# A two-block network in fp32: a head's rows come to all partitions by DMA and TensorE in place of GpSimd, and the merge's first branch is written three tiles ahead

## The chip, the cores and the metric

The kernel runs on one core of one Trainium2 chip. The metric is the device time of one execution in microseconds (us), as the median of several executions. Of the core's engines the text uses these names: PE (TensorE; PEld is its weight load), DVE (VectorE), ACT (ScalarE), POOL (GpSimd) and SP (SyncE, which here only issues DMAs).

## The reference

The reference is a two-block network over 512 tokens of width 1024, with 16 learned tokens put in front (528 columns in all). The change lies in the first block's token mixer, which has two branches from one input projection. Cut to them:

```python
y_a = gelu(s5_ssm(u, ...))                      # branch a: a state space model
y_a = y_a * sigmoid(y_a @ w_glu)
hb = mlstm_chunkwise(q, k, v, log_i, log_f)     # branch b: 4 heads of 128
hb = hb * rsqrt(mean(hb * hb, axis=-1) + eps) * g_head
y_b = hb * sigmoid(o)
merged = sigmoid(ga) * (y_a @ w_a) + sigmoid(gb) * (y_b @ w_b)
return x + rmsnorm(merged @ w_out, g_post)
```

In mlstm_chunkwise a score q.k of the tokens t and s is weighted by exp(F_t - F_s + log_i_s - m_t), F being the running sum of the log forget gates and m_t a running maximum; the result is divided by a normaliser by token.

## The kernel before, in words

All activations lie feature major: 128 features on the partitions, tokens along the free dimension. Products run in fp32r with each operand split into a high and a low half, so a product is three matmuls per 128 rows (`mm3`, lines 135 to 138, and `product`, lines 165 to 168). A chunk of weights (512 KB) is loaded by SP into one of three staging buffers (`wst`), copied to its high half by ACT (line 125) and to its low half by DVE (line 126), each with three buffers. PSUM banks for products come from `product_bank`: in phases with the extra pool in turns from that pool (tiles `mx`) and from the common one (tiles `mm`), else from the common one, every third time from the norms' bank (`rs`).

The mLSTM part (lines 793 to 835) treats the heads one after the other. `gate_rows` and `gate_scans` have already left, for the four heads, the negated running maximum in rows 0, 32, 64 and 96 of the tile `negm`. For a head, `mlstm_inputs` prepares q, k (convolution, tanh), v (transposed) and the output gate, and, as its last stage, has GpSimd copy the head's row of `negm` to all 128 partitions into the tile `nmb`, of which there is one (line 638). `mlstm_units` then works through eight pairs of a query range (258 or 256 columns) and a key tile: scores on PE; the decay as `nmb` plus a column per key on DVE (line 659), its exponential on ACT (line 660); where the key tile lies on the diagonal, a multiplication by a triangle on POOL (line 663); scores times decay on DVE (line 665); its split (lines 106 and 107); numerator and denominator on PE. The units' stages are woven with fillers: the products of the sixteen gate tiles and of the gated linear unit.

At the end, with two activations over the tile `rows` (lines 828 and 829), the norms' factors of the four heads stand in rows 0, 32, 64 and 96. For each head POOL copies its row to all partitions (line 832), DVE multiplies (line 834) and the result is split into `b2` (line 835). Then `merge`: for each of eight output tiles f it loads the chunk `w_ab[f]` and, for each of two token ranges, forms the product of branch a (from `a2`), its gating on DVE (line 893), the product of branch b (from `b2`), its gating, the sum of both on POOL (line 894) and the split (line 895). The loop is written tile by tile, a before b. After that come the inputs x, the bias rows of the second block (lines 1068 to 1078) and the product with `w_out`.

What is written is not the order in which the engines run: the framework's planner simulates the program and gives each engine a list in the order of the simulated times, keeping dependencies and buffers; each engine then works through its list in order, and so does SP with its DMAs. In the trace loads stand far ahead of their place in the text (the load of `rel`, line 1063, is issued at 213 us), and a tile waits for the release of the tile whose space it takes.

Of the kernel before, what the change touches and what calls it, by code (L numbers as in the profile page):

```python
# [49 lines left out]
# columns of the packed parameter vectors  # L50
# [13 lines left out]
class Net:  # L64
# [37 lines left out]
    def split(self, hi, lo, src, gain=None):  # L102
        """hi + lo = src * gain, each of 12 bits."""
        nc = self.nc
        if gain is None:
            nc.scalar.activation(hi, src, AF.Copy)
            nc.vector.tensor_tensor(lo, src, hi.bitcast(FT), OP.subtract)
        else:
            nc.scalar.activation(hi, src, AF.Copy, scale=gain)  # L109
            nc.vector.scalar_tensor_tensor(lo, src, gain, hi.bitcast(FT), OP.mult, OP.subtract)  # L110

    def weights(self, src, shape, own=None):
        """A chunk of weights [P, kt, cols] from DRAM as its two halves."""
# [16 lines left out]
    def mm3(self, ps, terms, start=True, stop=True):  # L130
        """ps (+)= sum of (ah + al)^T (bh + bl), leaving out al^T bl (2^-24 of the product)."""
# [8 lines left out]
    def project(self, w, c0, ranges, evac, m=P):  # L140
        """Columns c0.. of a weight chunk times the split activations, range by range."""
# [7 lines left out]
    def product(self, src, ranges, evac, m=P, after=None, own=None):  # L149
        """A chunk's product with the split activations as (load, pieces): evac(ps, t0, n) per range."""  # L150
# [23 lines left out]
    def product_bank(self):  # L174
        """A bank for a product: of the pool that all phases have, or in turns of that and more; in phases without
        wide norms, the norms' bank too, every third time."""
# [10 lines left out]
    def chain(self, jobs, last=None):  # L187
        """The pieces of jobs in order, each job's weights loaded one job ahead."""
# [8 lines left out]
    def log_exp_tables(self):  # L197
        """Of the function tables, those with both the logarithm and the exponential."""
# [8 lines left out]
    def next_input(self, act=None, extra=None, more=1):  # L207
        """Tiles for the next product's input, and for its tokens' factors; sums of squares in more parts where
        there's room for them."""
# [9 lines left out]
    def split_x(self, k, gname, t0, n):  # L219
        """Input tile k = x * g, split, and its part of the tokens' sums of squares."""  # L220
# [8 lines left out]
    def add_square(self, accs, x, k):  # L229
        """accs[k % len(accs)] (+)= x * x; the k-th of them."""  # L230
# [12 lines left out]
    def rstd(self, *a, **kw):  # L243
        """The steps of rstd_steps at once; returns the factors by token."""
# [4 lines left out]
    def rstd_wide(self, out, accs, t, width=DM):  # L249
        """out[:, t] = (sum over partitions of accs[..][:, t] / width + eps) ** -0.5 on every partition. One Newton  # L250
        step refines the tables' value."""
# [14 lines left out]
    def rstd_steps(self, pool, out, accs, n, width=DM, tag="rsr"):  # L266
        """out[:, t] = (sum over partitions of accs[..][:, t] / width + eps) ** -0.5 on every partition, for n
        tokens; and by token: [n / groups, groups]. One Newton step refines the tables' value."""
# [28 lines left out]
    def ssm_setup(self, pool, tmp):  # L297
        """Per state (partition: real or imaginary part, then state) and group: powers of lambda, the
        input matrix, and the rotations of the scan over chunks. A generator: lambda_bar, then the rest."""
# [56 lines left out]
        def cmul(orr, oi, ar, ai, br, bi, n):  # L356
            """(orr, oi) = a * b, with a of [P, n, NG] and b of [P, NG]."""
# [14 lines left out]
        # z = (lambda_bar - 1) / lambda  # L372
# [26 lines left out]
        # signed powers: al, be of the output side, qi of the input side  # L399
# [9 lines left out]
        # mag ** 8, and exp(i 8 theta c) as a product of two tables  # L409
# [26 lines left out]
    def ssm_tile(self, ft, ud, out):  # L436
        """One feature tile (8 groups) of the state space model as a generator: first its matrices,
        within a chunk (mt), from inputs to the chunk's state (q), from the state to outputs (pp); then
        2 gelu(y) to out, in the order of tokens."""
# [15 lines left out]
        # K[h', (lag, h)] of each group, and from it the block Toeplitz matrix  # L455
# [99 lines left out]
    def gate_rows(self, pool):  # L555
        """Rows 0, 32, 64, 96: the heads' running maximum (negated), exp(-2 m); and per key tile the
        columns a_s = log_i - F."""
# [14 lines left out]
    def gate_scans(self, pool, g8, li, zf):  # L572
# [21 lines left out]
        V.tensor_scalar(nm, nm, -1.0, None, OP.mult)  # L594
        ac = pool.tile([P, 5, 4], FT, name="acol")
# [7 lines left out]
    def mlstm_inputs(self, h, raws, ins):  # L603
        """q, k (convolved, split), v (by token, split) and tanh(o / 2) of one head, as a generator."""
# [32 lines left out]
        ins["m"] = self.hp.tile([P, L], FT, name="nmb")  # L637
        nc.gpsimd.partition_broadcast(ins["m"], self.negm[32 * h:32 * h + 1, :])

    def mlstm_units(self, h, ins, yb):  # L640
        """2 y_b of one head but for its norm's factor, and the factor's argument to a row: scores with
        their decays, a generator per key tile."""
# [54 lines left out]
    def mixer(self):  # L697
# [3 lines left out]
        with ExitStack() as es:  # L701
# [13 lines left out]
            with ExitStack() as e2:  # L715
# [4 lines left out]
                with tc.tile_pool(name="tmp0", bufs=1, side="right", reuse_waits="tile") as tmp:  # L720
# [26 lines left out]
                    # the factors are needed where a range's last piece ends  # L747
# [32 lines left out]
            def gate(f, out):  # L780
                """tanh(g / 2) of a gate's feature tile."""
# [11 lines left out]
            with ExitStack() as e2:  # L793
# [23 lines left out]
                load()  # L817
                for _ in prep(0):
                    pass
                units = []  # L820

                for h in range(4):
                    us = self.mlstm_units(h, ins[h], ybs[h])
                    units += ([prep(h + 1)] if h < 3 else []) + us
                self.weave([(units, fill)])
                # the heads' norms
# [1077 lines left out]
```

## Time and profile before

| what | value |
|---|---|
| device time, 3 runs | 1583.81, 1586.16, 1589.71 us; median 1586.16 us |
| profiled execution: its span, first to last instruction | 1585.8 us (the page lists no other time of it) |
| mean granted TensorE clock | 0.972 of full speed |
| busy: PE, DVE, ACT, POOL | 94%, 65%, 46%, 22% of the span |
| mLSTM with its fillers | about 217 to 377 us of the span |
| merge | about 377 to 430 us |

A line of the timeline gives the start in us from the span's start, the length in us, the engine, the line of the code, the operation, the tile written and those read, the shapes and a count of merged instructions; in square brackets stand the idle time of that engine just ahead, and what ended it ("issue": nothing that the profile shows). A PE row's length includes the pipeline's depth, so starts, not lengths, give its pace.

### The profile page before, as it was taken

The numbers are of one execution on the slowest core, as the hardware profiler recorded it, in microseconds if no ns is written. First come the engines' busy times: TensorE is split into PE (matmuls) and PEld (weight loads), VectorE is DVE, ScalarE is ACT, GpSimd is POOL, SyncE is SP. The second block draws the span as 40 slices with busy tenths as digits, with TensorE's granted clock in tenths as the row PEclk, the third lists the DMA queues.
The fourth block names the chain that finished last, engine by engine and source line by source line (L and its number), as shares of the span: only waits on it lengthen the run. The fifth ranks groups of instructions, "written<-read, shape, count | busy, mean of one in ns | idle before, by whom it ended". The sixth has DMA issues, their size and how long they took to land.

```text
span 1585.8 us, 24977 instructions
## 1 busy us (share of the span) xinstructions
PE 1485.1 (94%) x9745; PEld 1339.8 (84%) x9745; DVE 1031.2 (65%) x1960; ACT 722.4 (46%) x1396; POOL 341.0 (22%) x316
## 2 busy tenths in 40 slices
PE   5998998789998999999999999999889999999996
PEld 4988998778998999999999987878778888888886
DVE  8787877657777655555465687888888443344334
ACT  5233355446464533333455456666557441134332
POOL 4066720112343000000022354412343000000001
PEclk9998999989999999999999999999899999999998
DMA  5433331113645333233656322113230232323331
GB/s 187 95 97 104 80 107 50 54 41 120 213 146 160 107 93 94 93 95 91 190 162 197 119 67 67 52 56 107 81 107 28 93 93 94 93 93 94 93 93 54
DMA packets 65846, 160.86 MB, mean 101 GB/s; under 512 B 15032, under 2 KB 24488, under 8 KB 65600
## 3 DMA queue, kind: packets, MB, share of 16 engines
q1 hardware_dynamic: 64352, 156.65, 32.6%
q8 instruction: 76, 1.25, 0.3%
q0 software_dynamic: 288, 1.57, 0.3%
q10 hardware_dynamic: 1088, 1.05, 0.2%
q14 instruction: 42, 0.34, 0.1%
HBM read 152.84 MB, written 10.32 MB: 103 GB/s over the span
## 4 chain that ended last, share of the span: by engine, by line
PE 69%; DVE 18%; DMA 4%; ACT 4%; issue 4%; POOL 1%; SPq 0%; DVEq 0%; ACTq 0%; POOLq 0%
PE mm L135 6%; PE mm L138 6%; PE mm L136 6%; PE mm L165 6%; PE mm L168 6%; PE mm L167 6%; PE mx L168 5%; PE mx L165 5%; PE mx L167 5%; PE mx L135 2%; PE mx L136 2%; PE mx L138 2%; DVE wlo L126 2%; DVE xl L110 2%; PE mm L1324 1%
## 5 line engine op out<-in xcount | busy, mean ns | idle before, releaser
L126 DVE TENSOR_TENSOR wlo<-wst,whi 128x1024 fp32r<-128x1024 f32 (+2 forms) x227 | 283.2, 1249 | 197.4 <-ACT whi L125 121.6
L125 ACT ACTIVATE whi<-wst 128x1024 fp32r<-128x1024 f32 (+3 forms) x244 | 251.8, 1033 | 290.9 <-PE mm L136 94.6
L168 PE MATMUL mm<-xl,whi 128*128 128x256 f32 (+4 forms) x808 | 234.0, 315 | 0.3 <-DVE xl L110 0.3
L167 PE MATMUL mm<-xh,whi 128*128 128x256 f32 (+4 forms) x808 | 233.5, 314 | 0.2 <-DVE x L1614 0.2
L167 PE MATMUL mx<-xh,whi 128*128 128x512 f32 (+4 forms) x552 | 171.6, 332 | 8.1 <-ACT xh L109 7.5
L168 PE MATMUL mx<-xl,whi 128*128 128x512 f32 (+4 forms) x552 | 172.1, 332 | 3.2 <-DVE xl L110 3.2
L167 PEld LDWEIGHTS mm<-xh,whi 128*128 128x128 f32 (+1 forms) x808 | 154.1, 191 | 9.9 <-DVE x L1643 0.3
L168 PEld LDWEIGHTS mm<-xl,whi 128*128 128x128 f32 (+1 forms) x808 | 153.5, 190 | 10.3 <-issue 0.6
L165 PE MATMUL mm<-xh,wlo 128*128 128x256 f32 (+4 forms) x808 | 140.9, 314 | 0.0
L135 PE MATMUL mm<-hh,whi 128*128 128x256 f32 (+1 forms) x496 | 139.2, 311 | 0.0
L136 PE MATMUL mm<-hl,whi 128*128 128x256 f32 (+1 forms) x496 | 139.1, 310 | 0.0
L165 PEld LDWEIGHTS mm<-xh,wlo 128*128 128x128 f32 (+1 forms) x808 | 118.2, 190 | 9.7 <-issue 0.5
L167 PEld LDWEIGHTS mx<-xh,whi 128*128 128x128 f32 (+1 forms) x552 | 106.8, 193 | 17.7 <-ACT xh L109 7.7
L168 PEld LDWEIGHTS mx<-xl,whi 128*128 128x128 f32 (+1 forms) x552 | 106.7, 193 | 14.1 <-DVE xl L110 4.7
L165 PE MATMUL mx<-xh,wlo 128*128 128x512 f32 (+4 forms) x552 | 103.7, 329 | 0.0
L126 POOL TENSOR_TENSOR wlo<-wst,whi 128x1024 fp32r<-128x1024 f32 (+1 forms) x34 | 75.0, 2209 | 123.1 <-PE mm L138 38.3
L966 POOL TENSOR_TENSOR acc<-acc,osq 128x256 f32<-128x256 f32 (+1 forms) x26 | 25.0, 963 | 345.2 <-ACT osq L963 345.1
L135 PEld LDWEIGHTS mm<-hh,whi 128*128 128x128 f32 x496 | 93.5, 189 | 6.1
L136 PEld LDWEIGHTS mm<-hl,whi 128*128 128x128 f32 x496 | 93.6, 189 | 5.8
L165 PEld LDWEIGHTS mx<-xh,wlo 128*128 128x128 f32 (+1 forms) x552 | 84.9, 191 | 9.3 <-issue 0.2
L138 PE MATMUL mm<-hh,wlo 128*128 128x256 f32 (+1 forms) x496 | 83.6, 310 | 1.3 <-DVE wlo L126 1.3
L138 PEld LDWEIGHTS mm<-hh,wlo 128*128 128x128 f32 x496 | 70.5, 189 | 7.4 <-DVE wlo L126 1.7
(553 smaller groups left out, 3367.5 us busy)
## 6 DMA issues: line engine op xcount, KB each, us to landing
wst<-in_w_in_dram SPq DMA_DIRECT2D x52, 512.0 KB, 3.6
wst<-in_w_down_dram SPq DMA_DIRECT2D x32, 512.0 KB, 3.5
wst<-in_w_mup_dram SPq DMA_DIRECT2D x32, 512.0 KB, 3.5
wst<-in_w_mdown_dram SPq DMA_DIRECT2D x32, 512.0 KB, 3.8
wst<-in_w_gate_dram SPq DMA_DIRECT2D x22, 512.0 KB, 3.6
wst<-in_w_up_dram SPq DMA_DIRECT2D x22, 512.0 KB, 3.5
wst<-in_w_out_dram SPq DMA_DIRECT2D x20, 512.0 KB, 3.7
wst<-in_w_down_dram SPq DMA_DIRECT2D x16, 384.0 KB, 3.9
```

Source lines behind the costliest of these rows:

```text
L110: nc.vector.scalar_tensor_tensor(lo, src, gain, hi.bitcast(FT), OP.mult, OP.subtract)
L125: nc.scalar.activation(hi[:, 0:n], st[:, 0:n], AF.Copy)
L126: self.wlow.tensor_tensor(lo[:, 0:n], st[:, 0:n], hi[:, 0:n].bitcast(FT), OP.subtract)
L135: nc.tensor.matmul(ps, ah, bh, start=start and i == 0, stop=False)
L136: nc.tensor.matmul(ps, ah, bl, start=False, stop=False)
L138: nc.tensor.matmul(ps, al, bh, start=False, stop=stop and i == n - 1)
L165: nc.tensor.matmul(ps, wl[:, k], xh, start=False, stop=k == KT - 1)
L167: nc.tensor.matmul(ps, wh[:, k], xh, start=k == 0, stop=False)
L168: nc.tensor.matmul(ps, wh[:, k], xl, start=False, stop=False)
L966: nc.gpsimd.tensor_tensor(acc, acc, sq, OP.add)
L1324: nc.tensor.matmul(ps, wh[:, k], xh, start=k == 0, stop=False)
```

## The change

1. `gate_scans` also stores the four rows of `negm` to a DRAM tile `nmd`. The new function `decay_row` loads one head's row from there into all 128 partitions by one DMA on SP (264 KB written, 2112 bytes per partition). There are two such tiles, `nmb0` and `nmb1`; the loads for heads 0 and 1 are issued ahead of the first head's preparation, those of heads 2 and 3 at the start of their preparation. GpSimd's copy at line 638 is gone.
2. The heads' norms: for each head and each of the two token ranges, one fp32 matmul of a column of the identity, repeated, with the tile `rows` puts the head's row on all partitions of a PSUM bank (pool `pst`, two banks); DVE multiplies from there, and the split is done by range. GpSimd's copies at line 832 are gone.
3. `merge` is written as branch products: a of tiles 0, 1 and 2, then b of tile 0, and from there b of tile f and a of tile f + 2 in turn.

Comments are dropped, which shifts lines. The core of the diff:

```diff
+        self.nmd = self.dram.tile([4, L], FT, name="nmd")
+        nc.sync.dma_start(self.nmd, nm[0:P:32, :])
...
-        ins["m"] = self.hp.tile([P, L], FT, name="nmb")
-        nc.gpsimd.partition_broadcast(ins["m"], self.negm[32 * h:32 * h + 1, :])
+        ins["m"] = ins["mrow"]
+
+    def decay_row(self, h, ins):
+        t = ins["mrow"] = self.hp.tile([P, L], FT, name=f"nmb{h % 2}")
+        row = self.nmd[h]
+        self.nc.sync.dma_start(t, bass.AP(tensor=row.tensor, offset=row.offset, ap=[[0, P], [1, L]]))
...
+                for h in range(2):
+                    self.decay_row(h, ins[h])
                 for _ in prep(0):
                     pass
                 units = []
+                def prepare(h):
+                    if h > 1:
+                        self.decay_row(h, ins[h])
+                    yield from prep(h)
                 for h in range(4):
                     us = self.mlstm_units(h, ins[h], ybs[h])
-                    units += ([prep(h + 1)] if h < 3 else []) + us
+                    units += ([prepare(h + 1)] if h < 3 else []) + us
...
                 for h in range(4):
-                    rb = self.hp.tile([P, L], FT, name="nmb" if h % 2 else "cacc")[:, T0:L]
-                    nc.gpsimd.partition_broadcast(rb, self.rows[32 * h:32 * h + 1, T0:L])
-                    y = ybs[h][:, T0:L]
-                    V.tensor_tensor(y, y, rb, OP.mult)
-                    self.split(b2[h][0][:, T0:L], b2[h][1][:, T0:L], y, 0.5)
+                    for (t0, n) in TAIL:
+                        ps = self.pst.tile([P, 512], FT, name="st")[:, 0:n]
+                        nc.tensor.matmul(ps, self.ident[:, 32 * h:32 * h + 1].to_broadcast([P, P]),
+                                         self.rows[:, t0:t0 + n], start=True, stop=True)
+                        y = ybs[h][:, t0:t0 + n]
+                        V.tensor_tensor(y, y, ps, OP.mult)
+                        self.split(b2[h][0][:, t0:t0 + n], b2[h][1][:, t0:t0 + n], y, 0.5)
...
-        for f in range(KT):
-            wh, wl = self.weights(I["w_ab"][f], (8, P))
...
+        ws = {}
+        def branch(f, i):
+            if f not in ws:
+                ws[f] = self.weights(I["w_ab"][f], (8, P))
+            wh, wl = ws[f]
...
+                ps = self.product_bank()
+                self.mm3(ps[:, 0:n], self.terms((wh[:, 4 * i:4 * i + 4], wl[:, 4 * i:4 * i + 4]), 0, (a2, b2)[i],
+                                                t0, n, 4))
+                V.scalar_tensor_tensor(gs[i], gs[i], 1.0, ps[:, 0:n], OP.add, OP.mult)
+                if i:
+                    nc.gpsimd.tensor_tensor(gs[0], gs[0], gs[1], OP.add)
+                    self.split(mg[f][0][:, t0:t0 + n], mg[f][1][:, t0:t0 + n], gs[0], 0.5)
+        for f, i in [(0, 0), (1, 0), (2, 0), (0, 1)] + [
+                fi for f in range(1, KT) for fi in ((f, 1), (f + 2, 0)) if fi[0] < KT]:
+            branch(f, i)
```

## Rows read from the trace of the kernel before

**Rows 1.** The page: its head, three of the engines' busy times with share of the span and instructions, and the chain that ended last by engine.

```profile
span 1585.8 us, 24977 instructions
...
PE 1485.1 (94%) x9745; PEld 1339.8 (84%) x9745; DVE 1031.2 (65%) x1960; ACT 722.4 (46%) x1396; POOL 341.0 (22%) x316
...
PE 69%; DVE 18%; DMA 4%; ACT 4%; issue 4%; POOL 1%; SPq 0%; DVEq 0%; ACTq 0%; POOLq 0%
```

**Rows 2.** Busy time by stretch: the whole mLSTM stage and two stretches inside it. Columns: stretch, its length; busy us and instructions of PE, PEld, DVE, ACT, POOL; granted clock; DMA share; GB/s.

```profile
217.00:377.00 160.00, 139.74 (x1063) 127.88 (x1063) 109.45 (x234) 83.75 (x187) 17.38 (x24) 0.94 0.19 58
230.00:260.00 30.00, 30.00 (x243) 27.89 (x242) 26.23 (x52) 19.03 (x41) 2.96 (x4) 1.00 0.22 71
283.00:303.00 20.00, 20.00 (x158) 18.09 (x157) 15.56 (x32) 11.42 (x25) 1.87 (x2) 1.00 0.18 53
```

**Rows 3.** The timeline of POOL: GpSimd's four copies of a head's row and the instruction that follows each.

```profile
217.08 0.84 POOL L638 PARTITION_BROADCAST nmb<-negm  x1 [9.24 <-PE tr L538]
230.00 2.04 POOL L663 TENSOR_TENSOR dt<-dt,tri 16x2 f32<-16x2 f32 x2 [12.08 <-ACT dt L660]
...
264.73 1.05 POOL L638 PARTITION_BROADCAST nmb<-negm  x1 [5.93 <-DVE ql L110]
272.78 0.44 POOL L663 TENSOR_TENSOR dt<-dt,tri 128x128 f32<-128x128 f32 x1 [7.00 <-issue]
...
307.64 0.82 POOL L638 PARTITION_BROADCAST nmb<-negm  x1 [5.82 <-issue]
315.95 0.60 POOL L663 TENSOR_TENSOR dt<-dt,tri 128x128 f32<-128x128 f32 x2 [7.49 <-issue]
...
340.95 1.02 POOL L638 PARTITION_BROADCAST nmb<-negm  x1 [5.84 <-ACT sh L106]
349.03 0.44 POOL L663 TENSOR_TENSOR dt<-dt,tri 128x128 f32<-128x128 f32 x1 [7.07 <-issue]
```

**Rows 4.** The timeline of PE: the first matmul after each of its three long idle times in the stage.

```profile
274.00 0.47 PE L135 MATMUL num<-sh,vh 128*128 128x128 f32 x1 [5.36 <-ACT sh L106]
...
317.17 0.47 PE L135 MATMUL num<-sh,vh 128*128 128x128 f32 x1 [8.18 <-ACT sh L106]
...
349.86 0.58 PE L135 MATMUL st<-qh,kh 128*128 128x256 f32 x1 [5.41 <-DVE dt L665]
```

**Rows 5.** Busy time by stretch, as in rows 2: one stretch ahead of the first idle time, and the stretch behind each of the three.

```profile
262.00:268.30 6.30, 6.30 (x56) 6.09 (x55) 2.85 (x6) 2.19 (x5) 1.05 (x1) 1.00 0.21 78
274.00:279.40 5.40, 5.40 (x26) 5.40 (x27) 5.40 (x13) 4.65 (x12) 2.42 (x2) 0.50 0.23 59
317.20:320.30 3.10, 3.10 (x15) 3.10 (x16) 3.06 (x9) 2.94 (x7) 0.92 (x2) 0.50 0.00 0
349.90:354.40 4.50, 4.50 (x22) 4.50 (x23) 3.80 (x11) 3.88 (x11) 0.93 (x3) 0.50 0.00 0
```

**Rows 6.** DVE's decays of a head from the tile `nmb` (timeline of DVE): the first of head 0, the last of head 0, the first of head 1.

```profile
228.88 0.60 DVE L659 TENSOR_SCALAR dt<-nmb,acol 16x258 f32<-16x258 f32 x2
...
262.04 0.27 DVE L659 TENSOR_SCALAR dt<-nmb,acol 128x128 f32<-128x128 f32 x1
...
274.14 0.34 DVE L659 TENSOR_SCALAR dt<-nmb,acol 16x258 f32<-16x258 f32 x1
```

**Rows 7.** DMA issues of the whole run by their tiles: size of one, and median us from issue to landing.

```profile
x<-in_x_dram SPq DMA_DIRECT2D x16, 264.0 KB, 6.7
...
bias<-ed SPq DMA_DIRECT2D x16, 256.0 KB, 2.9
...
uc<-ud SPq DMA_DIRECT2D x4, 264.0 KB, 4.0
```

**Rows 8.** The heads' norms (timelines of ACT, POOL and DVE): the last activation over the rows, the first copy of a row, the next instruction on POOL after the fourth copy, and the end of the last split.

```profile
380.42 0.63 ACT L829 ACTIVATE rows<-rows 128x514 f32<-128x514 f32 x1
...
381.19 0.82 POOL L832 PARTITION_BROADCAST cacc<-rows  x1 [9.42 <-ACT rows L829]
...
392.79 2.35 POOL L894 TENSOR_TENSOR sga<-sga,r 128x258 f32<-128x258 f32 x2 [7.12 <-issue]
...
389.19 0.68 DVE L110 SCALAR_TENSOR_TENSOR xl<-yb,xh 128x514 fp32r<-128x514 f32 x1
```

**Rows 9.** The timeline of PE in the same time and in the merge: an fp32 matmul (two instructions), the first matmuls of branch a of tiles 0 and 2 (in `mx` banks) and of branch b of tile 0, and the idle times.

```profile
376.91 0.59 PE L688 MATMUL st<-sqn,ones 128*1 128x256 f32 x2 [1.30 <-ACT sqn L682]
377.43 0.39 PE L135 MATMUL mx<-xh,whi 128*128 128x258 f32 x1
...
383.48 0.39 PE L135 MATMUL mx<-xh,whi 128*128 128x258 f32 x1
...
383.94 0.40 PE L135 MATMUL mm<-xh,whi 128*128 128x258 f32 x2
...
392.23 0.39 PE L135 MATMUL mm<-xh,whi 128*128 128x258 f32 x1 [0.84 <-DVE r L893]
...
405.03 0.39 PE L135 MATMUL mm<-xh,whi 128*128 128x256 f32 x1 [1.23 <-DVE r L893]
...
410.07 0.39 PE L135 MATMUL mm<-xh,whi 128*128 128x258 f32 x1 [1.23 <-DVE r L893]
```

**Rows 10.** The timeline of ACT in the merge: a wait for the second block's memory, and the next copy of weights.

```profile
403.62 0.51 ACT L109 ACTIVATE ya<-mem,par 128x256 fp32r<-128x256 f32 x1 [3.56 <-DMA mem<-in_mem_dram]
...
406.71 1.05 ACT L125 ACTIVATE whi<-wst 128x1024 fp32r<-128x1024 f32 x1
```

More of the change, by code (lines that the diff above doesn't have):

```diff
@@ L884, in merge @@
         free = [8, 9, 10, 11, 12, 13, 14, 15, 0, 1, 2, 3, 4, 5, 6, 7]
-        for f in range(KT):
-            wh, wl = self.weights(I["w_ab"][f], (8, P))
-            mg.append([self.ring.tile([P, L], FR, name=f"r{i}") for i in free[2 * f:2 * f + 2]])
+        ws = {}
[4 more added lines that the diff above has]
+            if i:
+                mg.append([self.ring.tile([P, L], FR, name=f"r{j}") for j in free[2 * f:2 * f + 2]])
             for (t0, n) in TAIL:
                 gs = (sga[f][:, t0 - T0:t0 - T0 + n], gb[f][:, t0 - T0:t0 - T0 + n])
-                for i, ys in enumerate((a2, b2)):
-                    ps = self.product_bank()
-                    self.mm3(ps[:, 0:n], self.terms((wh[:, 4 * i:4 * i + 4], wl[:, 4 * i:4 * i + 4]), 0, ys, t0, n, 4))
-                    V.scalar_tensor_tensor(gs[i], gs[i], 1.0, ps[:, 0:n], OP.add, OP.mult)
-                nc.gpsimd.tensor_tensor(gs[0], gs[0], gs[1], OP.add)
-                self.split(mg[f][0][:, t0:t0 + n], mg[f][1][:, t0:t0 + n], gs[0], 0.5)
+                ps = self.product_bank()
+                self.mm3(ps[:, 0:n], self.terms((wh[:, 4 * i:4 * i + 4], wl[:, 4 * i:4 * i + 4]), 0, (a2, b2)[i],
+                                                t0, n, 4))
+                V.scalar_tensor_tensor(gs[i], gs[i], 1.0, ps[:, 0:n], OP.add, OP.mult)
+                if i:
+                    nc.gpsimd.tensor_tensor(gs[0], gs[0], gs[1], OP.add)
[3 more added lines that the diff above has]
+            branch(f, i)
         self.xp = self.pool(self.ctx, "xp", side="right")
```

## The prediction

> **What bounds the kernel now.** I read the page first: PE is busy for 94% of the span and makes up 69% of the chain that ended last [rows 1]. So a change gains only where PE stands still or is slowed, or where it takes matmuls away; this one takes none away. Next I read the busy time by stretch. In the mLSTM stage, 160 us long, PE is busy for 139.74 us and the mean granted clock is 0.94, while two stretches inside it show PE busy all the time at clock 1.00, with DVE at 26.23 of 30 us [rows 2]. So when nothing goes wrong PE is the bound here, DVE is next, at 87%, and some 20 us of the stage are holes. The timeline of PE shows the holes: 5.36, 8.18 and 5.41 us, each ended by a step of a head's scores and not by a lack of weights [rows 4]. The timeline of POOL names the cause. GpSimd's copies of a row take only 0.8 to 1.05 us, but the next instruction, the triangle on a diagonal tile, starts 7.00, 7.49 and 7.07 us after the copy, and "issue" says that it waited for nothing that the profile shows. Ahead of the same three copies stand another 5.8 to 5.9 us of idle time [rows 3]. POOL is unable to work for some 14 us each time a head's copy passes, PE's fillers cover the first half, and PE then waits: triangle, scores times decay, split, numerator. The copy of head 0 is harmless: the next triangle, 12.08 us later, was waiting for its exponential anyway [rows 3].
>
> **What it costs, part by part.**
>
> *The copies of the decay rows go (a gain).* Without a copy among them POOL's triangles start when their exponential is there, so the three holes close: 5.36 + 8.18 + 5.41 = 18.95 us [rows 4]. Each hole has a sequel. For 5.40, 3.10 and 4.50 us behind it the granted clock is 0.50, the 1.2 GHz level, after PE had stood still; 26 + 15 + 22 = 63 matmuls take 13.0 us there. Ahead of the first hole, at 1.00 (2.4 GHz), 56 take 6.30 us, or 0.1125 us each, so the 63 would take 7.1 us, and 5.9 us are lost [rows 5]. Together 24.85 us. This counts on nothing else being late in the holes' place. Next in line is DVE: its 109.45 us in the stage [rows 2] would fall into 160 - 24.85 = 135 us, 81%, less than the 87% at which PE is shown without a hole. I therefore take the full 24.85; the lower end is half of it (the second rival).
>
> The rule of the Trainium skill that bears on this is in "GPSIMD Engine Reference", section "Instruction dispatch": the first call to a freshly loaded GpSimd kernel pays about 6 us (5.95 measured) for loading code, with no instruction to see. The 5.8 to 5.9 us ahead of the copies agree with it; for the way back, which makes the holes, it has no price, and the rows have 7.0 to 7.5. Were that 6 us too, the holes would be some 3.6 us smaller in sum and the result, as an estimate by that page, about 1567; the rows decide.
>
> *The rows arrive by DMA.* One store of four rows and four loads of 264 KB are added on SP's queue. Transfers of 256 to 264 KB land in 2.9 to 6.7 us here [rows 7]. The first use is at 228.88, and a head's decays spread over 33 us, 228.88 to 262.04, with the next head's starting at 274.14 [rows 6]; with two tiles a load has the whole time of a head to land. Behind a load in SP's list stand weights; they come 3 to 7 us later at the worst, once per head, and three staged chunks cover that (a chunk is 2 x 24 matmuls, 5.4 us of PE at 0.1125). So I cost this at nothing. From below it is also nothing, for PE has no other hole that an earlier row would close; from above, one landing in full sight, 6.7 us. I take 0, the value of a load that is asked for a head ahead. If the cover is gone, the third rival tells what it costs.
>
> *The heads' norms by TensorE.* Before, the rows are ready at 380.42 + 0.63 = 381.05, the last split ends at 389.87 [rows 8], and PE fills the time with branch a of tiles 0, 1 and 2, begun at 377.43, and the first of branch b [rows 9]. The copies there cost PE little: POOL's next work comes 7.12 us after the fourth [rows 8], but PE's own hole about that time is only 0.84 us [rows 9]. Added are 8 fp32 matmuls; the one like them in the trace, 256 columns, holds PE from 376.91 to 377.43, 0.52 us [rows 9], so 4.2 us of new PE work on the engine that is the bound. DVE's multiplications stay the same in sum (half the width, twice the count) and lie beside PE. A wait is added as well: the norms use the two `pst` banks until the last multiplication, at about 389 again, and the pool for the merge's `mx` banks is opened after that pool is closed, in its place, so two of the three `mx` banks may come free late. Branch a of tile 2 starts 6.05 us after that of tile 0 [rows 9], which is four products at 1.5 us. If only four of the six a-products find a bank, PE has 6.0 + 4.2 = 10.2 us of work for the 12.4 us from 377.43 to 389.87 and stands still for 2.2; if all six do, there is no hole. Behind a waiting product in PE's list stands everything, so this hole would be in full sight.
>
> *The merge's order.* The text now runs branch a three tiles ahead. But the trace shows that the planner had done so already: a of tile 2 starts at 383.48, ahead of b of tile 0 at 383.94 [rows 9]. I give this part nothing of its own. PE's holes in the merge, 0.84 + 1.23 + 1.23 = 3.3 us [rows 9], come with ACT, which stands 3.56 us for a load of the second block's memory and copies the next weights only after that [rows 10]; nothing in the change moves that load. At best they close, at worst they stay.
>
> *Sum of the two.* Best: 4.2 of work less the 3.3 of holes, and less the 1.30 ahead of 376.91 [rows 9], -0.4. Worst: 4.2 + 2.2 = 6.4. I take +2.5, nearer to the measured 4.2 less half of the holes.
>
> **Total.** The profiled span is 1585.8 us [rows 1], 0.4 under the median of the runs, 1586.16, and no other time of that execution is listed; I carry the 0.4 along. 1585.8 - 24.85 + 2.5 + 0.4 = 1563.85: forecast 1564 us, faster by 1.4%.
>
> **Rivals.**
>
> First: the merge runs better too. If POOL's return at 392.79 [rows 8] was holding the chain of sums and splits, and the new order keeps PE fed past ACT's wait, the holes close: 1585.8 - 24.85 - 0.4 + 0.4 = 1561 by my terms, and another 4 to 5 us if b of tile 0 begins with its splits by range rather than after 389.87: 1556. For it: branch b needs only one range at a time now. Against: DVE has the same work to do first.
>
> Second: half of the gain only. Behind each copy stood not one late triangle but DVE's convolutions and splits of the next head, held up with it; if they had to be done in the open, each hole would leave half. 24.85 / 2 = 12.4: 1585.8 - 12.4 + 2.5 + 0.4 = 1576 us, or 1574 where the merge costs little. For it: in the 5.40 us behind the first hole DVE is busy throughout [rows 5]. Against: the stretches at 87% without a hole [rows 2].
>
> Third, the other side: SP's queue stands. The planner brings loads far forward, and the row of head 2 needs `nmb0`, which head 0 reads until 262.04 [rows 6]. Put into SP's list when head 0 starts, at about 230, it would hold every load of weights behind it for 32 us. Three staged chunks last PE 3 x 5.4 = 16 us, so PE would stand 16 us; the same for head 3; with 2 us of slow clock each (5.9 over three holes) that is 36 us lost against 22 won: 1600 us. It decides from some 28 us of standing per load (16 covered and 12, half the gain, on top). For it: SP works in order. Against: the planner knows the release in its simulated times, and the text asks for that load only when head 0's units are well on.
>
> Fourth: no change. The holes belong to the place and not to the copy, as when the head's own chain takes that long; 1586 + 2.5. Against: the first copy, with nothing behind it, and the idle time that names no one.
>
> **How the numbers follow.** The forecast with its own range, 1557 to 1571, has 0.58; the better merge (below 1557) 0.14; half of the gain (1571 to 1578) 0.18; no change 0.06; the standing queue 0.04. The range that leaves out about 2 in 10 reaches from 1553 to 1576. A change of 0.5%, 7.9 us, is about what a measurement tells from none: faster by more has the first two cases and nearly all of the third, 0.88; within it 0.08; slower 0.04.
>
> **What would show it.** Right: no idle time over 3 us on POOL ended by "issue" between 217 and 377; PE without a hole over 1 us there, granted clock 1.00, and the stage, up to the last score of head 3, shorter by 23 to 25 us; eight fp32 matmuls of 0.52 us behind the rows' activations; the merge, up to the first product with `w_out`, 0 to 6 us longer. Wrong: PE's holes there with another name behind them (a decay, a DMA, weights); SP waiting for a decay's release with weights behind; a merge longer by over 7 us, or holes elsewhere in the span, where the planner's new order moves work that the change does not touch.

## The result and the profile after

The changed kernel takes 1561.93 us in the median against 1587.01 before. The ratio of all their runs is 0.9859, 95% interval 0.9839 to 0.9878 (the quotient of the two medians alone, 0.9842, lies near its lower end). The forecast was 1564, with 1557 to 1571 as its own range. The profiled execution of the changed kernel took 1567.67 us, the longest of its four (the others 1561.04 to 1562.42), so its rows are compared by stretches; a second profile of the same kernel (run `changed_again` below, median 1561.63) stands beside it. The milestones, each the start of a matmul in the timeline of PE, in us:

| | before | after | after, again |
|---|---|---|---|
| last fp32 matmul of head 3 (end of the mLSTM) | 376.91 | 350.88 | 350.96 |
| first product with `w_out` (end of the merge) | 429.52 | 404.23 | 403.63 |
| norm behind `w_out`, second range | 495.12 | 473.70 | 470.01 |
| end of the span | 1585.8 | 1564.4 | 1559.0 |

The mLSTM ends 26 us earlier, a little more than the 23 to 25 that the prediction gave as its sign, and the merge is 0.1 to 0.7 us longer. The busy time of the changed kernel over the mLSTM (columns as in [rows 2]):

```profile
217.00:353.00 136.00, 135.02 (x1075) 123.14 (x1074) 110.14 (x236) 85.90 (x191) 13.15 (x20) 1.00 0.26 83
```

Against [rows 2], PE is idle for 1 us of the stage in place of 20, and its granted clock is 1.00 in place of 0.94. DVE does the same 110 us of work in 136, 81%.

POOL's timeline in the changed kernel, at the places where heads 1, 2 and 3 begin:

```profile
262.34 0.84 POOL L670 TENSOR_TENSOR dt<-dt,tri 128x128 f32<-128x128 f32 x1 [5.11 <-ACT dt L667]
...
295.03 0.50 POOL L670 TENSOR_TENSOR dt<-dt,tri 128x128 f32<-128x128 f32 x1 [2.77 <-ACT dt L667]
...
321.10 0.46 POOL L670 TENSOR_TENSOR dt<-dt,tri 128x128 f32<-128x128 f32 x1 [5.47 <-ACT dt L667]
```

The idle time ahead of every triangle (now line 670) is ended by the triangle's exponential; the "issue" of [rows 3] is gone. The decay rows' DMAs, SP's timeline and the landing time that the view of the tile `nmd` gives for the four loads:

```profile
215.63 0.33 SPq L645 DMA_DIRECT2D nmb<-nmd  x1
216.48 0.42 SPq L645 DMA_DIRECT2D nmb<-nmd  x1
260.76 0.33 SPq L645 DMA_DIRECT2D nmb<-nmd  x1
294.24 0.33 SPq L645 DMA_DIRECT2D nmb<-nmd  x1
...
DMA to landing us min/median/max: 3.4/3.5/3.6
```

The third load is asked for at 260.76, when head 0 is done with the tile, and not at 230 as the rival of a standing queue had it. No engine waits for a load; SP itself stands 1.6 us in all, in two waits, until the decays let a tile go.

The timeline of PE between head 3 and the merge (line 695 was 688, line 847 is the norms' matmul; "x8" is four products of two instructions, and the row at 360.48 is the last of the eight):

```profile
346.49 0.28 PE L135 MATMUL mm<-xh,whi 128*128 128x256 f32 x1
...
350.88 0.59 PE L695 MATMUL st<-sqn,ones 128*1 128x256 f32 x2 [0.98 <-ACT sqn L689]
...
355.07 2.35 PE L847 MATMUL st<-rows,ident 128*128 128x258 f32 x8 [0.38 <-ACT rows L843]
...
360.48 0.59 PE L847 MATMUL st<-rows,ident 128*128 128x256 f32 x2
...
362.46 0.28 PE L135 MATMUL mx<-xh,whi 128*128 128x258 f32 x1
...
372.72 0.39 PE L135 MATMUL mx<-xh,whi 128*128 128x258 f32 x1 [1.49 <-ACT whi L125]
```

Two things are to be seen. Until 362 all products of branch a stand in `mm` banks; the first in an `mx` bank starts only behind all eight norm products. And a product of branch a already stands at 346.49, ahead of head 3's last fp32 matmul; before, the first one stood behind it, at 377.43, in an `mx` bank [rows 9]. The time is as forecast, but these rows speak against the prediction's account of the second and the third part, so the runs take the change apart.

### The profile page after: what moved, and what is told of

It is laid out like the page before. It is cut to its first block, busy times and chain, and to the rows that moved or that the text cites. A ratio compares the mean times of both kernels' runs of the same rounds, so it can differ in the third digit from the quotient of the medians.

```text
span 1564.4 us, 25002 instructions
## 1 busy us (share of the span) xinstructions
PE 1479.6 (95%) x9761; PEld 1334.2 (85%) x9761; DVE 1032.0 (66%) x1968; ACT 724.1 (46%) x1400; POOL 335.5 (21%) x308
## 3 DMA queue, kind: packets, MB, share of 16 engines
q10 hardware_dynamic: 1088, 1.05, 0.2%
## 4 chain that ended last, share of the span: by engine, by line
PE 54%; DVE 10%; ACT 3%; issue 1%; DMA 1%; POOL 0%; DVEq 0%; ACTq 0%; POOLq 0%
PE mm L135 6%; PE mm L138 5%; PE mm L136 5%; PE mm L165 5%; PE mm L168 5%; PE mm L167 5%; PE mx L165 4%; PE mx L168 4%; PE mx L167 4%; DVE xl L110 2%; PE mx L135 2%; PE mx L138 2%; PE mx L136 2%; DVE ptl L107 1%; PE tr L1208 1%
## 5 line engine op out<-in xcount | busy, mean ns | idle before, releaser
L993 POOL TENSOR_TENSOR acc<-acc,osq 128x256 f32<-128x256 f32 (+1 forms) x26 | 25.2, 969 | 344.6 <-ACT osq L990 344.6
```

What stands on the lines that cost most here:

```text
L993: nc.gpsimd.tensor_tensor(acc, acc, sq, OP.add)
```

## The experiments

### Each part alone, and the parts in pairs

`rows_only`, `norms_only` and `merge_only` are the kernel before with one part of the diff; `rows_norms` and `rows_merge` are the changed kernel with one part put back. What is put back for the merge and for the norms:

```diff
-        for f, i in [(0, 0), (1, 0), (2, 0), (0, 1)] + [
-                fi for f in range(1, KT) for fi in ((f, 1), (f + 2, 0)) if fi[0] < KT]:
-            branch(f, i)
+        for f in range(KT):
+            wh, wl = self.weights(I["w_ab"][f], (8, P))
...
-                    for (t0, n) in TAIL:
-                        ps = self.pst.tile([P, 512], FT, name="st")[:, 0:n]
-                        nc.tensor.matmul(ps, self.ident[:, 32 * h:32 * h + 1].to_broadcast([P, P]),
...
+                    nc.gpsimd.partition_broadcast(rb, self.rows[32 * h:32 * h + 1, T0:L])
```

> The kernel before with the first part alone: the decay rows come by loads from DRAM; the heads' norms stay with GpSimd's copies and the merge keeps its old order. Theory A (the prediction's step): the three holes of 5.36, 8.18 and 5.41 us and the 5.9 us at half clock behind them go, 24.85 us in all, so about 1562 us. Rival B (half of each hole was other work that is now done in the open): about 1575 us. In the trace, by A, the last fp32 matmul of head 3 ends at about 352 us and POOL has no idle time over 3 us ended by issue before the norms; the merge takes about 52.6 us as before.

> The kernel before with the second part alone: the heads' norms by eight fp32 matmuls, the decay rows still by GpSimd's copies, the old order of the merge. Theory A (the prediction's sum): 8 x 0.52 = 4.2 us of PE work less some of the merge's holes, +2.5 us, so about 1588.7 us. Theory B (the banks): the norms use the two pst banks to the end, two of the three mx banks come free only behind them, and with the old order all first products of the merge ask for these banks, so PE does the norms in full sight: up to +6.4 us, about 1592 us. Rival C (the copies' outage mattered here too and goes): 1586 us or less. Told apart by PE's rows between the last fp32 matmul of head 3 and the first product of the merge in an mx bank.

> The kernel before with the third part alone: the merge's first branch three tiles ahead in the text; decay rows and norms by GpSimd's copies. Theory A (the prediction's step: the planner had put branch a of tile 2 ahead of branch b of tile 0 already): no change, 1586 us, within 2 us. Rival B (the new order keeps PE fed past ACT's wait for the memory): the merge's holes of 0.84, 1.23 and 1.23 us go, about 1583 us or less.

> The changed kernel with the merge's old order: parts one and two without part three. Theory A (the prediction gave the merge's order nothing): equal to the changed kernel, 1562 us, within 2 us. Theory B (parts two and three belong together: in the old order all branch-a products that could run ahead of the norms ask for mx banks, which come free only behind the norms; in the changed kernel the second ranges of branch a use mm banks and run during head 3's end): slower than the changed kernel by 3 to 6 us, 1565 to 1568 us, with PE holes around the norms' matmuls.

> The changed kernel with the heads' norms given back to GpSimd's copies: parts one and three without part two. Theory A (the parts add up: rows alone 1560.8 against 1586.0, the merge's order alone 1580.9 against 1586.0): 1560.8 - 5.1 = 1555.7 us, about 6 us faster than the changed kernel, with no hole over 1 us of PE between head 3's last fp32 matmul and the first product with w_out. Rival B (without the decay copies the merge has another state, and its order is worth nothing there): 1561 us, as rows alone.

Measured, medians in us, with the ratio to before (1586.02 for the first four, 1586.08 for the last) and its interval:

| run | us | ratio |
|---|---|---|
| `rows_only` | 1560.80 | 0.9843 (0.9830 to 0.9855) |
| `norms_only` | 1593.11 | 1.0048 (1.0035 to 1.0062) |
| `merge_only` | 1580.89 | 0.9972 (0.9961 to 0.9982) |
| `rows_norms` | 1565.58 | 0.9872 (0.9859 to 0.9885) |
| `rows_merge` | 1556.46 | 0.9813 (0.9794 to 0.9832) |

The rows are worth 25.2 us. The norms cost 7.1 alone, 4.8 on top of the rows (1565.58 - 1560.80) and 5.5 on top of rows and merge (1561.93 - 1556.46). The merge's order gains 5.1 alone, 4.3 on top of the rows and 3.7 on top of rows and norms. So theory A of `rows_only` and of `rows_merge` came out, and theory B of `norms_only` (1 us beyond its bound of 1592), of `merge_only` and of `rows_norms`. Within what such medians tell, the parts add up, and the changed kernel is not the best of them: without the norms on PE it is 5.5 us faster by the medians, and the two intervals of the ratio, 0.9794 to 0.9832 and 0.9839 to 0.9878, don't meet.

What does the merge's order gain by? Busy time by stretch, from head 3's last third to the first product with `w_out`: first the kernel before, then `merge_only`.

```profile
366.40:377.40 11.00, 9.70 (x71) 7.64 (x70) 9.14 (x22) 6.92 (x19) 1.38 (x2) 1.00 0.23 63
377.40:429.50 52.10, 48.40 (x387) 46.28 (x387) 40.25 (x75) 24.54 (x45) 20.85 (x22) 1.00 0.68 209
```

```profile
366.10:377.80 11.70, 11.16 (x83) 9.09 (x82) 9.14 (x22) 6.92 (x19) 1.38 (x2) 1.00 0.26 77
377.80:424.80 47.00, 46.01 (x375) 44.72 (x375) 39.14 (x74) 24.37 (x46) 21.91 (x21) 1.00 0.67 226
```

The two stretches together went from 63.1 to 58.7 us, and PE's idle time in them from 63.1 - 58.1 = 5.0 to 58.7 - 57.2 = 1.5. Of the 3.5 us, 2.7 lie in the merge and 0.8 at the end of head 3. Twelve matmuls, one product of branch a, moved from the merge into the end of head 3. The old text takes its banks in turns, a from `mx` and b from `mm`, and `mx` is opened when the scores' banks are closed: nothing of branch a could run before head 3's end. The new text takes a's first range from `mx` and its second from `mm`, and the second ranges fill PE's gaps at the end of head 3. The waits of PE, first before (366 to 430), then `merge_only` (366 to 425):

```profile
PE mm L135 <- DVE r L893: 3.3, 3, 1.2
PE st L688 <- ACT sqn L682: 1.3, 1, 1.3
```

```profile
PE mx L136 <- DVE xl L110: 1.0, 3, 0.5
PE st L688 <- ACT sqn L682: 0.5, 1, 0.5
```

With branch a ahead, no product waits for the gating (line 893) to give its bank back. Rival B of `merge_only` has it right. The new text changes two things at once, how far branch a runs ahead and which banks it takes; no run has the new order with the old turns, so how much is due to either is not shown.

### Which banks the norms take

`rows_norms` shows the price of the old order with the norms on PE. Its timeline of PE, and its busy time in that stretch:

```profile
349.43 1.01 PE L695 MATMUL st<-sqn,ones 128*1 128x256 f32 x2 [2.00 <-ACT sqn L689]
353.62 2.97 PE L847 MATMUL st<-rows,ident 128*128 128x258 f32 x6 [3.18 <-ACT rows L843]
```

```profile
349.40:361.60 12.20, 8.86 (x28) 5.82 (x28) 6.63 (x19) 6.20 (x10) 0.00 (x0) 0.61 0.64 228
```

PE stands 3.18 us for the rows' activations with no other work, and the granted clock of the stretch is 0.61. Two runs move the norm products to other banks, `old_order_acc_banks` from `rows_norms` and `norms_acc_banks` from the changed kernel; `norms_dma` brings the norms' rows through DRAM as the decay rows.

```diff
-                        ps = self.pst.tile([P, 512], FT, name="st")[:, 0:n]
+                        ps = self.pacc.tile([P, 512], FT, name="den" if t0 > T0 else "num")[:, 0:n]
```

```diff
+                nc.sync.dma_start(nrd, self.rows[0:P:32, T0:L])
...
-                        nc.tensor.matmul(ps, self.ident[:, 32 * h:32 * h + 1].to_broadcast([P, P]),
-                                         self.rows[:, t0:t0 + n], start=True, stop=True)
...
+                    nc.sync.dma_start(rb, bass.AP(tensor=nr.tensor, offset=nr.offset, ap=[[0, P], [1, L - T0]]))
```

> The changed kernel with the merge's old order (run rows_norms, 1565.6 us) and the eight norm products in the numerator's and denominator's banks. Theory A (in rows_norms the hole of 3.18 us ahead of the norms and the half clock about it come from the mx banks that wait for the scores' banks): branch a starts at once behind head 3's last fp32 matmul, the hole is gone, and the time falls by 3 to 5 us, to 1561 to 1563 us. Rival B (the hole comes with ACT's table loads and the rows' activations, whatever the banks): the hole stays, 1565.6 us within 1 us.

> The changed kernel with the eight norm products in the banks of the numerator and denominator instead of the scores' two banks, so that the mx banks, which take the scores' place, come free at head 3's end. Theory A (banks hold branch a back): products of branch a in mx banks start before the norms' matmuls, the 0.38 and 0.81 us holes there go, and the time is 1 to 3 us under the changed kernel, 1559 to 1561 us. Rival B (the norms cost their 4.2 us of PE work and nothing else once the merge runs three tiles ahead): no change from 1562 us.

> The changed kernel with the heads' norms brought to all partitions as the decay rows are: one store of the four rows to DRAM and four loads that repeat them, no matmul and no GpSimd copy. Theory A (PE's 4.2 us and the banks are the norms' price; the DMA's way of some 6 to 8 us is covered by branch a of three tiles): as rows and merge order without the norms, about 1555 to 1557 us. Rival B (the store and the loads take longer than branch a covers, and weights wait behind them in SP's list): PE stands behind the norms, 1560 us or more.

Measured, in the order of the three expectations: 1560.34 us (5.2 less than `rows_norms`), 1563.99 and 1563.80. The timeline of PE in `old_order_acc_banks`:

```profile
350.14 0.59 PE L695 MATMUL st<-sqn,ones 128*1 128x256 f32 x2 [1.98 <-ACT sqn L689]
350.67 0.39 PE L135 MATMUL mx<-xh,whi 128*128 128x258 f32 x1
...
354.34 0.70 PE L847 MATMUL num<-rows,ident 128*128 128x258 f32 x2
```

Branch a starts in an `mx` bank behind head 3's last matmul, and the norms' products come among it without a hole. So the 3.18 us were the banks' doing, and in the old order the norms on PE then cost nothing against `rows_only` (1560.34 to 1560.80); that the idle time of the old order's merge takes them in is likely, but no run shows it. In the new order the same edit gains nothing, and theory A of `norms_acc_banks` fails: the time is 1563.99 (1559.51 to 1565.03) against 1561.93. Branch a does start ahead of the norms in `mx` banks there and the hole of 0.38 us goes, but the one of 0.8 us stays, and PE's wait for weights that ACT splits late, 1.49 us in the changed kernel's first profile and 0.8 in its second, is longer:

```profile
PE mx L135 <- ACT whi L125: 2.1, 1, 2.1
```

`norms_dma` takes the norms off PE, but its way is longer than PE's other work. Of PE and of ACT in that run:

```profile
364.07 0.58 PE L135 MATMUL mx<-xh,whi 128*128 128x258 f32 x1 [5.52 <-ACT xh L109]
```

```profile
363.38 1.27 ACT L109 ACTIVATE xh<-yb 128x514 fp32r<-128x514 f32 x2 [8.62 <-DVE yb L851]
```

ACT's first split of branch b comes 363.38 - 354.77 = 8.6 us behind the rows' last activation (354.13 + 0.64), and PE stands 5.52 us: rival B, but for its weights, for which PE does not wait here. What a load hides a head ahead, it does not hide where its row is just being made.

### What made the holes of the mLSTM

`triangle_on_dve` leaves GpSimd's copies of the decay rows and takes away what stood behind them; `unused_copies` adds to the changed kernel copies that nobody needs.

```diff
-                nc.gpsimd.tensor_tensor(dt[0:ns, 0:m], dt[0:ns, 0:m], self.tri[0:ns, o:o + m], OP.mult)
+                nc.vector.tensor_tensor(dt[0:ns, 0:m], dt[0:ns, 0:m], self.tri[0:ns, o:o + m], OP.mult)
```

```diff
         ins["m"] = ins["mrow"]
+        if h:
+            nc.gpsimd.partition_broadcast(self.hp.tile([P, 64], FT, name="unused"), vh[0:1, 1, 0:64].bitcast(FT))
```

> The kernel before, with GpSimd's copies of the decay rows as they are, and the triangle of the diagonal tiles multiplied by DVE instead of GpSimd. Theory A (the holes are GpSimd's way back from a copy to the next triangle, not the copy or a head's place): with nothing behind the copies that PE waits for, the three holes and the half clock behind them go, about 1561 us plus at most 3 us for DVE's added products. Rival B (the holes belong to the place: a head's own chain of scores, decay and split takes that long): they stay with DVE's names on them, 1586 us.

> The changed kernel with three copies by GpSimd added that nothing reads: a row of 64 numbers of v to all partitions, one for each of heads 1 to 3, among the triangles where the old copies stood. Theory A (the switch is the price, not the copied size and not that somebody needs the copy): each copy has 5.8 to 5.9 us of idle time ahead of it and 7.0 to 7.5 us behind it, and PE's holes of some 5 to 8 us come back wherever a triangle stands behind; 10 to 25 us slower, 1572 to 1587 us. Rival B (the holes came from the whole row's copy and from decays waiting for it): a copy of 64 columns that nobody waits for costs nothing, 1562 us.

Measured: 1565.90 us (0.9876, 0.9861 to 0.9892) and 1566.32 us (0.9878, 0.9859 to 0.9897); before was 1585.29 beside them. In `triangle_on_dve` PE's waits between 217 and 430 hold no decay and no triangle any more, and of the scores' steps only 0.3 us for a split; its longest:

```profile
PE st L688 <- ACT sqn L682: 1.4, 1, 1.4
PE st L688 <- DVE yb L686: 1.4, 1, 1.4
PE mm L136 <- DVE xl L110: 0.5, 1, 0.5
...
PE num L136 <- DVE sl L107: 0.3, 1, 0.3
```

The holes of [rows 4] are gone while the copies, and the one tile `nmb` that they write, are still there: rival B falls. Head 3 ends at 354.76, 22.2 us earlier than before and 3.6 later than in `rows_only` (351.17). DVE has 20 products (5.2 us) more, and PE waits 1.42 us for it at 331.56; that this makes the whole difference is not shown.

The run takes away more than the way back from a copy, though: GpSimd then has nothing but copies to do in the stage, and the way to a copy no longer holds anything up either. The last decay of head 0 there (DVE) and the copy behind it (POOL):

```profile
263.14 0.28 DVE L659 TENSOR_SCALAR dt<-nmb,acol 128x128 f32<-128x128 f32 x1
...
263.59 0.81 POOL L638 PARTITION_BROADCAST nmb<-negm  x1 [44.90 <-DVE dt L659]
```

The copy starts 0.17 us after the decay that frees its tile, without 5.8 us of its own; the next two, at 297.18 and 325.13, start 0.16 us after theirs. How the two ways share the price is read from the kernel before. The exponentials for the three late triangles of [rows 3] (timeline of ACT):

```profile
263.47 0.29 ACT L660 ACTIVATE dt<-dt 128x128 f32<-128x128 f32 x1
...
303.93 0.29 ACT L660 ACTIVATE dt<-dt 128x128 f32<-128x128 f32 x1
...
340.13 0.31 ACT L660 ACTIVATE dt<-dt 128x128 f32<-128x128 f32 x1 [0.97 <-DVE dt L659]
```

They end at 263.76, 304.22 and 340.44, so the triangles are 9.0, 11.7 and 8.6 us late: 7.0 to 7.5 us each by the way back, 0.8 to 1.05 by the copy, and the rest, 0.5 to 3.4, by what is left of the way to the copy. In `unused_copies`, POOL's timeline:

```profile
251.70 0.55 POOL L641 PARTITION_BROADCAST unused<-vh  x1 [5.76 <-ACT dt L669]
259.99 1.30 POOL L672 TENSOR_TENSOR dt<-dt,tri 128x128 f32<-128x128 f32 x1 [7.74 <-ACT sh L106]
...
277.45 0.37 POOL L641 PARTITION_BROADCAST unused<-vh  x1 [5.94 <-ACT sh L106]
285.63 0.44 POOL L672 TENSOR_TENSOR dt<-dt,tri 128x128 f32<-128x128 f32 x1 [7.81 <-issue]
...
314.19 0.37 POOL L641 PARTITION_BROADCAST unused<-vh  x1 [5.80 <-ACT vh L106]
322.82 0.45 POOL L672 TENSOR_TENSOR dt<-dt,tri 128x128 f32<-128x128 f32 x1 [8.26 <-ACT dt L669]
```

Copies of 64 columns, 0.37 to 0.55 us long, have the idle times of the 528-column ones, 5.8 to 5.9 us ahead; behind the second, 7.81 us end with "issue". The price is the switch between a copy and other work, not the size. But only there did PE come to need the triangle, by its timeline and its busy time around it:

```profile
286.45 0.58 PE L135 MATMUL st<-qh,kh 128*128 128x256 f32 x1 [3.01 <-DVE dt L674]
```

```profile
283.00:286.40 3.40, 0.44 (x4) 0.13 (x2) 0.29 (x2) 0.00 (x0) 0.44 (x1) 0.84 0.00 0
286.40:292.00 5.60, 5.55 (x27) 5.48 (x28) 5.56 (x13) 5.07 (x12) 0.00 (x0) 0.50 0.00 0
```

One hole of 3 us with 5.6 us at half clock behind it: theory A's mechanism, at one copy of three; at the other two PE shows no hole, as at the copy of head 0 in [rows 3]. By the medians the kernel is 4.4 to 4.7 us slower (1566.32 against 1561.93 and 1561.63), less than half of the least that theory A gave. That price is not sure: the four runs lie between 1562.88 and 1568.86, and the ratio's interval overlaps those of the changed kernel.

### The rest of the span, and the memory's loads

> The changed kernel once more, unaltered, beside the other runs. Theory A (the 4.7 us that ACT stands for a load of the next projection's weights, and PE's hole and half clock behind it, belong to the one profiled execution, whose time was the slowest of four): median 1561 to 1562.5 us, and in this profile the stretch from the first product with w_out to the second norm behind it takes about 66 us, as before, not 69.5. Rival B (the change moves that load): 69 us again.

> The kernel before with four tiles in place of two for the loads of the second block's memory. Theory A (the merge's holes of 1.23 us at 405 and 410 us come from these loads: ACT waits for one, DVE's split behind ACT, and behind that in DVE's list the gating that frees PE's bank): the two holes go, the merge takes 50 instead of 52.6 us, and the time is about 1583 to 1584 us. Rival B (the holes come from the old order's banks alone): no change, 1586 us within 1 us. Either way the merge's new order, which closes the same holes, is not tried here.

`changed_again`: 1561.63 us. Where the next projection begins, the first profile of the changed kernel has these rows of ACT and PE and this busy time:

```profile
459.93 1.06 ACT L125 ACTIVATE whi<-wst 128x1024 fp32r<-128x1024 f32 x1 [4.72 <-DMA wst<-in_w_xv_dram]
...
461.68 0.58 PE L135 MATMUL mm<-ya,whi 128*128 128x256 f32 x1 [2.61 <-ACT osq L990]
...
458.00:467.00 9.00, 6.39 (x37) 6.30 (x36) 3.82 (x9) 4.53 (x8) 0.00 (x0) 0.65 0.58 193
```

and the second:

```profile
458.88 1.06 ACT L125 ACTIVATE whi<-wst 128x1024 fp32r<-128x1024 f32 x1 [4.05 <-DMA wst<-in_w_xv_dram]
...
460.63 0.39 PE L135 MATMUL mm<-ya,whi 128*128 128x256 f32 x1 [0.64 <-ACT osq L990]
...
458.00:467.00 9.00, 8.36 (x71) 8.28 (x71) 5.29 (x11) 4.42 (x8) 0.00 (x0) 0.96 0.56 178
```

ACT's wait is in both, 4.0 to 4.7 us. PE's hole is 2.61 us in one and 0.64 in the other; the stretch about it runs at 0.65 of the clock in one and at 0.96 in the other, 37 matmuls against 71. The stretch from the first product with `w_out` to the second norm took 69.5 and 66.4 us (65.6 before): 3 us belong to that one execution, under 1 us to the change.

`memory_four_tiles`:

```diff
-            mem = mp.tile([P, MEM], FT, name="mem", bufs=2)
+            mem = mp.tile([P, MEM], FT, name="mem", bufs=4)
```

1585.75 us against 1585.29, ratio 1.0001 (0.9990 to 1.0012). Its waits of PE in the merge:

```profile
PE mx L135 <- DVE sga L893: 0.9, 2, 0.6
PE mm L135 <- DVE r L893: 0.7, 1, 0.7
```

The two holes of 1.23 us are gone and the merge of this profile takes 50.8 us, not 52.6; the median does not show it. So the loads of the memory do make those holes, but by the median what `merge_only` gains is not to be had by mending them. Why 1.8 us of the trace are not in the median stays open.

## Why the prediction was right, and where it was not

**The bound.** PE without holes at clock 1.00, DVE at 81%, was forecast and is what the stage shows.

**The copies of the decay rows.** Forecast 24.85 us, measured 25.2 by `rows_only`; in its trace head 3 ends 376.91 - 351.17 = 25.7 us earlier. The cause, GpSimd's switching between copies and triangles, is shown by `triangle_on_dve`, which takes the triangles away, and at one place by `unused_copies`, which brings copies back. The prediction put the holes to the way back alone; that is most of it, and the way to the copy adds 0.5 to 3.4 us to the delay of each triangle. The rival of half the gain falls: DVE's work found its place. The Trainium skill's page "GPSIMD Engine Reference", section "Instruction dispatch", has about 6 us for the first call of a freshly loaded kernel. The 5.76 to 5.94 us ahead of the small copies agree with that in length; that code is loaded in them no row shows. The prediction's estimate by that page, which set the way back at 6 us too and so the holes 3.6 us smaller, does not hold: that would leave this part some 21 us, and it measured 25.2.

**The DMA rows at nothing.** Right: 3.4 to 3.6 us to landing, asked for a head ahead, and no engine waits for them. SP does stand for a tile's release, which the prediction named as a sign of being wrong, but for 1.6 us in all and not for 32 at each of two loads: the rival of the standing queue falls.

**The norms by TensorE.** The eight products are there at 4.2 us in sum, as forecast. What they cost the kernel was sized too small: 4.8 on top of the rows, 5.5 on top of rows and merge, 7.1 alone. The hole for late banks, bounded at 2.2 us, is real: 3.18 us in `rows_norms` and 3.60 in `norms_only`, with clock lost behind it. The changed kernel is spared it only by the third part.

**The merge's order.** This step failed. It gave the new order nothing of its own, because the planner had put branch a ahead already, and [rows 9] do show that for tile 2 against tile 0's branch b. But those rows also show branch a in `mx` banks, its first product at 377.43, behind head 3's last fp32 matmul and not ahead of it, and three products that wait for the gating. With the new text one product of branch a runs before head 3's end and no product waits for the gating: 3.7 to 5.1 us, not nothing. The lead and the banks' turns change together, and their shares stay open. The gain is of the first rival's kind, without its 4 to 5 us more from splits by range. The prediction's best case, which closes the merge's 3.3 us of holes and the 1.30 ahead of head 3's last fp32 matmul, had the size of this gain; it did not see that the new order closes them.

**The sum.** +2.5 was forecast for norms and merge together: 4.2 of work less half of the merge's 3.3 us of holes. By the runs it is +4.8 - 3.7 = +1.1 (1561.93 - 1560.80). The cost was 0.6 us too small, the gain 2.0 us too small, and 1.4 are left; the forecast lies 2 us above the measured time. It was right for the right reason in its large term. That the small ones came so near is partly luck: the two errors have opposite signs, and the gain stood in the sum as half of holes that nothing in the change was said to close.

## What to carry to other kernels

Where the bound engine has no slack, work moved onto it costs its full length (4.2 us of matmuls cost 4.8 to 5.5 here), and a copy on another engine that has the time is cheaper even with 14 us of switching around it, as long as nothing waits for that engine meanwhile: the best version here, `rows_merge`, keeps GpSimd for the norms and takes it away only from among the triangles. Before an order in the text is given nothing, look which buffers its instructions ask for; in a pool taken by turns a new order also deals out the banks anew, and with them what can run early. A change of several parts that hits its forecast says little of the parts until each has been run alone.

## What the runs showed of the hardware that was not expected

GpSimd's idle time about a copy does not depend on its size: 5.76 to 5.94 us ahead of 64 columns as 5.8 to 5.9 ahead of 528, and 7.81 us behind where nothing else held the next instruction. The way to a copy costs nothing where GpSimd has nothing else to do: after 44.90 us without work a copy started 0.17 us after the decay that it waited for. And the same program at the same place lost 2.61 us in one execution and 0.64 in another to the same late load; the clock in the stretch about it was 0.65 and 0.96.
